# Modulation weights with 256 columns of all four chunks in a piece, and layer 1's second and third group at the end of layer 0's experts

## The chip, the cores and the metric

The kernel runs on one core of a Trainium2 chip. Its engines are TensorE (PE in the profile; PEld is its weight load), VectorE (DVE), ScalarE (ACT), GpSimd (POOL) and SyncE (SP), which here issues nearly all DMAs. The metric is device time in microseconds (us). Before the change it is 2171.39 us, the median of three runs (2170.97 to 2172.95).

## The reference

Two layers of a transformer-like block work on 256 latent tokens and 256 context tokens of 1024 channels. Only the latents come out, so layer 1 computes queries for them alone. Everything is float32.

```python
for l in range(2):
    sh1, sc1, g1, sh2, sc2, g2 = split(silu(c) @ w_mod[l] + b_mod[l], 6)      # w_mod[l]: [1024, 6144]
    csh1, ..., cg2             = split(silu(c_ctx) @ w_mod[l] + b_mod[l], 6)  # the same weights, the context's vector
    h = layer_norm0(x) * (1 + sc1) + sh1                     # context tokens with csc1, csh1
    z = h @ w_in[l] + b_in[l]                                # columns for three mixers and their gates
    y = (sum over attention, GLA, neighbourhood of sigmoid(gate) * (branch @ w_br)) @ w_out[l]
    x = layer_norm(alpha * x + g1 * y)
    h2 = layer_norm0(x) * (1 + sc2) + sh2
    x = layer_norm(alpha * x + g2 * moe(h2))                 # 32 experts, two of them for each token
```

The change concerns the first two lines: a product of two vectors (c and c_ctx) with 25 MB of weights a layer, whose six results of 1024 columns scale, shift and gate the tokens. sh1 and sc1 are needed at the start of a layer, the others from its out_norm on.

## The kernel before

Tokens lie on the partitions in tiles of 128: four tiles in layer 0, two query tiles in layer 1. A layer runs through norm_T (normalisation, transposition, modulation), two GLA pairs (each for two heads of the gated linear attention), attention, neighbourhood attention, merges, out_norm, routing, the experts, a loop for tokens beyond the experts' slots, and final_norm.

**Modulation.** `modulation(l, groups)` makes 2048 of a layer's 6144 columns, called a group: four chunks of 512 columns. Group 0 holds shift and scale of the first norm, groups 1 and 2 the rest. The two vectors stand in `sT` as the 32-column stationary operand (30 columns are zero), and chunk j's result goes to rows 32 j to 32 j + 31 of one PSUM bank `mod`, that is to one of four column quarters of TensorE. The weights come in pieces of [128, 1024], 512 KB each, 16 for a group (eight steps over the 1024 rows, two halves). A piece holds 512 columns of two chunks, so each step's first piece serves quarters 0 and 1, the second 2 and 3. In the trace a float32 product is two instructions. Then VectorE adds the bias (`mg`, line 500), TensorE transposes `mg` (`modT`, line 503), VectorE takes columns from it (`mU`, line 517), and `mg` of groups 1 and 2 is stored to device memory as `md` (line 520), from which rows are read later (line 529). Called with the tag "tmod", the same tiles have the names `tmod` and `tmodT`.

**Where the groups stand.** Layer 0: group 0 at the start, groups 1 and 2 with the first and the second GLA pair. Layer 1: group 0 at the end of layer 0's out_norm, group 1 behind layer 1's norm_T, group 2 with its second GLA pair. In a GLA pair the scores G are made in six steps, between which VectorE works (`Sd`, line 732); other TensorE work fills the gaps.

**The end of layer 0.** Each expert has six tiles of 1 MB of weights; they come through six "ew" buffers and two "ewb" buffers. The last experts' second products Y (line 1414) and the combines `cb` (lines 1428 and 1429) are followed by sums on VectorE and GpSimd (lines 1431 and 1432, tile `ct` from two buffers). Then `overflow` reads a count and runs a loop over as many blocks (line 1545); with the inputs here it runs no block. All engines meet at the loop's head. Behind it come final_norm (lines 1589 to 1600), with its loads `lgb`, and layer 1.

**What sets the order.** Each engine runs its instructions in a fixed order, and so does SyncE with its DMAs. The order is made when the program is built, by a scheduler that follows the order of the source and may move work forward where its own estimate finds a gap. Nothing is moved across the loop's head. A tile from a pool waits until the instructions that use the buffer's former tile are done.

Of the kernel before, what the change touches and what calls it, by code (L numbers as in the profile page):

```python
# [21 lines left out]
NL = 2  # L22
# [5 lines left out]
# columns of w_in  # L28
A_Q, A_K, B_Q, B_K, B_V, B_R, B_A, C_Q, C_K, C_V, GATE = 0, 512, 768, 1024, 1280, 1792, 2304, 2336, 2848, 3360, 3872

# the order in which the mixers' weights stream in, one [128, 1024] piece each
# [27 lines left out]
# columns of the per-partition biases  # L59
# [9 lines left out]
# sections of the constants  # L69
# [9 lines left out]
# ranks of the experts of layer 0, by load but for experts 0 and 1, whose weights come in early:  # L79
# with 128 slots, with 64, the others with 32; the order of their halves of 128 slots  # L80
# [29 lines left out]
def groups(l):  # L110
    """The experts (in layer 0 by rank of their load) that share 256 slots, in two halves of one, two or four experts"""
# [10 lines left out]
def _constants():  # L122
# [5 lines left out]
    i = np.arange(128)  # L128
# [14 lines left out]
    # slots of the experts by rank  # L143
# [15 lines left out]
    # pairs of tokens of a block of 64 whose highest different bit is the level's  # L159
# [5 lines left out]
def _layout(inp):  # L165
    """The arrays of setup_inputs() as the program reads them."""
# [6 lines left out]
    # w_mod: [layer, group of four 512-column chunks, k tile, half of the group][partition][2 chunks x 512]  # L173
    wm = g["w_mod"].reshape(NL, 8, 128, 3, 2, 1024)
    o["wmod"] = np.ascontiguousarray(wm.transpose(0, 3, 1, 4, 2, 5))
# [8 lines left out]
    # branches in the order in which they are merged: gla, attention, neighbourhood  # L184
# [42 lines left out]
    # the relative bias of every (query, key), outside of the window a constant; context keys have none  # L227
# [12 lines left out]
    # experts: [layer, expert][partition][six pieces of 2048]  # L240
# [9 lines left out]
class _Prog:  # L250
# [3 lines left out]
    # ---- tiles  # L254
# [14 lines left out]
    def rsqrt(self, v, w, tmp=None):  # L269
        """v ** -0.5 by Newton's method"""  # L270
# [18 lines left out]
    def split(self, src, hi, lo, eng=None):  # L289
        """hi + lo = src, exactly, each with 12 significant bits"""  # L290
        self.nc.scalar.copy(hi, src)  # L291
        (eng or self.nc.vector).tensor_tensor(lo, src, hi.bitcast(F32), op=ALU.subtract)  # L292

    def stats(self, x):
        """mean and 1 / sqrt(var + eps) of x [128, 1024]"""
# [9 lines left out]
    def norm0(self, x, xh, total=None):  # L305
        """xh = layer_norm0(x), both [128, 1024]; with the sums of x, ScalarE makes those of its squares"""
# [15 lines left out]
    def stats_all(self, xs, apart=False):  # L322
        """stats of tiles together: columns of means, of 1 / sqrt(var + eps), and of the opposites of their products"""
# [25 lines left out]
    def norm_quick(self, x, out, g, b):  # L349
        """out = layer_norm0(x) * g + b, on VectorE alone, and the sums of its rows; x is overwritten"""  # L350
# [7 lines left out]
    def norm(self, x, out, g, b, last=None):  # L358
        """layer_norm0(x) * g + b, in two steps"""
# [4 lines left out]
    # ---- streams of weights  # L364
    def raw(self, l):
        """A place for weights as they come in; the first ones of layer 1 can't wait for the tokens that use the others"""
# [17 lines left out]
    def projT(self, l, n, ntok):  # L384
        """[128 columns of w_in, tokens] = w^T h^T"""
# [7 lines left out]
    def projM(self, l, names, kper, width, tiles, sub=None):  # L393
        """[tokens, columns of w_in] for the token tiles, one bank each"""
# [17 lines left out]
    # ---- constants  # L412
# [42 lines left out]
    def open(self, name, side, tags):  # L455
        """A pool that shares its place with the one that follows it on the same side"""
# [6 lines left out]
    @contextmanager  # L463
    def later(self, n=400):
        """What is traced here gives way to the next n instructions"""
        self.tc.cur_priority += n
        yield
        self.tc.cur_priority -= n

    # ---- modulation  # L470
    def modulation(self, l, groups, tag="raw", tag2="b2", ps="mod"):
        """[128, 512] of group g: row 32 j + s holds 512-column chunk 4 g + j for the latents (s = 0) and the context (s = 1)"""
# [11 lines left out]
        for g in groups:  # L484
            p = self.ps(ps)
            for k in range(8):
                if tag == "ew":
                    raw = self.t([128, 2, 1024], tag, name="wmod")
                    raws = [raw[:, h] for h in range(2)]
# [1221 lines left out]
```

## Time and profile before

| | before |
|---|---|
| time, median of 3 runs | 2171.39 us |
| profiled execution, span | 2169.8 us |
| TensorE busy | 1989.3 us (92%) |
| VectorE / ScalarE / GpSimd busy | 968.1 / 561.9 / 272.2 us |
| modulation products `mod` / `tmod`, busy | 75.0 / 20.0 us |
| modulation pieces loaded | 96 of 512 KB |

For the profiled execution the span is the only time of its own; what the runs time beyond it is the difference to their median, 1.6 us. Shares of busy time are means over stages with different limits, so a change in one stage is read from that stage's rows.

### The profile page before, as it was taken

Reading aid. Unit: us, or ns where it says so; the run is one execution under the profiler, and the core shown is the slowest. Engines: PE = TensorE matmul, PEld = TensorE weight load, DVE = VectorE, ACT = ScalarE, POOL = GpSimd, SP = SyncE. Lnnn points to the kernel's source line nnn. Section 1 sums busy time; section 2 is a strip of 40 time slices with the busy share of each in tenths; the row PEclk is TensorE's granted clock in tenths of the full one; section 3 lists DMA queues with packets and bytes.
Section 4 is the critical chain, followed back from the end, with each engine's and each line's share of the span. In section 5 each row is a group of like instructions: output and inputs, shape, how many; then the busy total and the mean of one; then the engine's idle time right before and its main releaser. Section 6 shows DMA issues by size and latency. Waiting matters only on the chain. (4 is left out here: it accounts for less than half of the span.)

```text
span 2169.8 us, 28061 instructions
## 1 busy us (share of the span) xinstructions
PE 1989.3 (92%) x10749; PEld 1179.2 (54%) x10749; DVE 968.1 (45%) x2236; ACT 561.9 (26%) x992; POOL 272.2 (13%) x260
## 2 busy tenths in 40 slices
PE   5999999999998898989899598999996999999995
PEld 2676766777885353445253165786795433333321
DVE  4676765564388131222022765766648222221213
ACT  3443334343333000000000254444543111010000
POOL 1322100011110010111011222100020000000000
PEclk9999999999999999999999798999997999999998
DMA  7436212223328899999998723632466999999995
GB/s 289 164 121 218 78 59 69 93 83 96 126 79 334 367 420 421 371 385 421 419 369 370 270 85 112 197 118 74 139 207 250 387 421 423 421 423 422 421 422 222
DMA packets 113987, 562.41 MB, mean 259 GB/s; under 512 B 13302, under 2 KB 14838, under 8 KB 72120
## 3 DMA queue, kind: packets, MB, share of 16 engines
q1 hardware_dynamic: 113272, 558.85, 66.9%
q8 instruction: 87, 1.43, 0.3%
q10 hardware_dynamic: 576, 1.70, 0.2%
q14 instruction: 52, 0.43, 0.1%
HBM read 557.36 MB, written 3.15 MB: 258 GB/s over the span
## 5 line engine op out<-in xcount | busy, mean ns | idle before, releaser
L1506 PE MATMUL h<-ew,XT 128*64 128x512 f32 (+2 forms) x2048 | 478.3, 611 | 40.0 <-DMA ew<-in_ew_dram 39.8
L1506 PEld LDWEIGHTS h<-ew,XT 128*64 128x64 f32 (+2 forms) x2048 | 146.6, 135 | 326.3 <-issue 248.8
L1414 PE MATMUL Y<-ew,aT 128*64 128x512 f32 (+2 forms) x1024 | 252.4, 598 | 10.1 <-DMA ew<-in_ew_dram 7.9
L292 DVE TENSOR_TENSOR wlo<-raw,whi 128x1024 fp32r<-128x1024 f32 (+1 forms) x140 | 178.9, 1278 | 139.6 <-ACT whi L291 138.4
L1432 POOL TENSOR_TENSOR x<-x,ct 128x512 f32<-128x512 f32 x82 | 105.0, 1307 | 1003.5 <-DVE ct L1431 879.8
L380 PE MATMUL pT<-hThi,whi 128*128 128x512 f32 (+1 forms) x576 | 202.9, 352 | 1.5 <-ACT whi L291 0.8
L291 ACT CAST whi<-raw 128x1024 fp32r<-128x1024 f32 (+1 forms) x140 | 145.4, 1039 | 226.5 <-PE pT L381 116.2
L382 PE MATMUL pT<-hThi,wlo 128*128 128x512 f32 (+1 forms) x576 | 202.3, 351 | 0.2 <-DVE wlo L292 0.2
L381 PE MATMUL pT<-hTlo,whi 128*128 128x512 f32 (+1 forms) x576 | 202.1, 351 | 0.0
L1403 DVE SCALAR_TENSOR_TENSOR act<-h,s,sl 128x512 f32<-128x512 f32 x30 | 22.5, 751 | 325.4 <-PE h L1506 270.5
L1414 PEld LDWEIGHTS Y<-ew,aT 128*64 128x64 f32 (+2 forms) x1024 | 76.0, 133 | 151.0 <-issue 125.7
L807 DVE TENSOR_TENSOR Yl<-Y,Yh 128x512 fp32r<-128x512 f32 x60 | 41.4, 690 | 257.2 <-ACT Yh L806 254.1
L806 ACT CAST Yh<-Y 128x512 fp32r<-128x512 f32 x60 | 35.2, 587 | 462.5 <-PE Y L1414 462.5
L380 PEld LDWEIGHTS pT<-hThi,whi 128*128 128x128 f32 x576 | 109.5, 190 | 22.4 <-issue 4.1
L382 PEld LDWEIGHTS pT<-hThi,wlo 128*128 128x128 f32 x576 | 109.5, 190 | 16.2 <-issue 2.9
L381 PEld LDWEIGHTS pT<-hTlo,whi 128*128 128x128 f32 x576 | 109.6, 190 | 15.2 <-issue 3.0
L380 PE MATMUL pM<-whi,hThi 128*128 128x512 f32 (+1 forms) x304 | 110.7, 370 | 3.6 <-ACT qTkT L645 1.9
L381 PE MATMUL pM<-wlo,hThi 128*128 128x512 f32 (+1 forms) x304 | 111.8, 369 | 0.0
L382 PE MATMUL pM<-whi,hTlo 128*128 128x512 f32 (+1 forms) x304 | 111.7, 368 | 0.0
L495 PE MATMUL mod<-wmod,sT 128*32 128x512 f32 x320 | 75.0, 624 | 23.4 <-DVE s L343 14.8
L1407 ACT COPY aT<-aT 128x512 f32<-128x512 f32 x30 | 17.6, 586 | 292.7 <-PE aT L1406 292.7
L1383 PE MATMUL XT<-OH,h2hi 128*128 128x256 f32 x352 | 89.1, 290 | 0.0
(363 smaller groups left out, 3093.4 us busy)
## 6 DMA issues: line engine op xcount, KB each, us to landing
ew<-in_ew_dram SPq DMA_DIRECT2D x326, 1024.0 KB, 13.8
raw<-in_w_dram SPq DMA_DIRECT2D x145, 512.0 KB, 3.7
ew<-in_ew_dram SPq DMA_DIRECT2D x116, 512.0 KB, 13.5
wmod<-in_wmod_dram SPq DMA_DIRECT2D x96, 512.0 KB, 6.1
nb<-in_nb_dram SPq DMA_DIRECT2D x32, 256.0 KB, 3.8
g<-md SPq DMA_DIRECT2D x12, 256.0 KB, 7.6
row<-in_ln_dram SPq DMA_DIRECT2D x4, 512.0 KB, 4.9
lgb<-in_ln_dram SPq DMA_DIRECT2D x4, 512.0 KB, 12.0
```

The source lines that it names most:

```text
L291: self.nc.scalar.copy(hi, src)
L292: (eng or self.nc.vector).tensor_tensor(lo, src, hi.bitcast(F32), op=ALU.subtract)
L380: mm(out, lh, rh, start=start, stop=False)
L381: mm(out, lh, rl, start=False, stop=False)
L382: mm(out, ll, rh, start=False, stop=stop)
L495: nc.tensor.matmul(p[32 * j:32 * j + 32, :], self.sT[:, k, :], raws[j // 2][:, 512 * (j % 2):512 * (j % 2) + 512], start=k == 0, stop=k == 7)
L806: self.nc.scalar.copy(hi, src)
L807: self.nc.vector.tensor_tensor(lo, src, hi.bitcast(F32), op=ALU.subtract)
L1383: mm(p[:, w * j:w * j + w], self.h2s[t][part][:, 128 * k:128 * k + 128], OH[:, t], start=t == 0 and part == 0, stop=t == T - 1 and part == 1)
L1414: mm(y[m * i:m * i + m, :], aT[:, 128 * f + m * i:128 * f + m * i + m], w2(f, n, i), start=f == 0, stop=f == 3)
L1432: (nc.vector if last and n else nc.gpsimd).tensor_tensor(self.x1[t][:, ns], self.x1[t][:, ns], tmp, op=ALU.add)
L1506: mm(h[m * i:m * i + m, :], XTs[dp][:, k, 128 * pr + m * i:128 * pr + m * i + m], w[i, 2 * q + k // 4][k % 4], start=k == 0, stop=k == 7)
```

## The change

Three things change, and line numbers from 487 on grow by two or three. The layout of `wmod` in device memory: a piece now has 256 columns of each of the four chunks. `modulation` runs over 16 such pieces, first the eight with the left halves of the chunks, then those with the right halves, with four products of 256 columns each. And layer 1's groups 1 and 2 leave their places and are made together behind layer 0's experts, in front of the overflow loop, with their weights in "ew" buffers (two pieces to a buffer) and bias and sum in "ct" buffers.

```diff
-    wm = g["w_mod"].reshape(NL, 8, 128, 3, 2, 1024)
-    o["wmod"] = np.ascontiguousarray(wm.transpose(0, 3, 1, 4, 2, 5))
+    wm = g["w_mod"].reshape(NL, 8, 128, 3, 4, 2, 256)
+    o["wmod"] = np.ascontiguousarray(wm.transpose(0, 3, 5, 1, 2, 4, 6)).reshape(NL, 3, 2, 8, 128, 1024)
...
         for g in groups:
             p = self.ps(ps)
-            for k in range(8):
+            for i in range(16):
+                h, k = i // 8, i % 8
                 if tag == "ew":
-                    raw = self.t([128, 2, 1024], tag, name="wmod")
-                    raws = [raw[:, h] for h in range(2)]
+                    if k % 2 == 0:
+                        both = self.t([128, 2, 1024], tag, name="wmod")
+                    raw = both[:, k % 2]
                 else:
-                    raws = [self.t([128, 1024], tag if isinstance(tag, str) else tag[2 * k + h], name="wmod") for h in range(2)]
-                for h in range(2):
-                    nc.sync.dma_start(raws[h], self.a["wmod"][l, g, k, h])
+                    raw = self.t([128, 1024], tag if isinstance(tag, str) else tag[i], name="wmod")
+                nc.sync.dma_start(raw, self.a["wmod"][l, g, h, k])
                 for j in range(4):
-                    nc.tensor.matmul(p[32 * j:32 * j + 32, :], self.sT[:, k, :], raws[j // 2][:, 512 * (j % 2):512 * (j % 2) + 512],
+                    nc.tensor.matmul(p[32 * j:32 * j + 32, 256 * h:256 * h + 256], self.sT[:, k, :], raw[:, 256 * j:256 * j + 256],
                                      start=k == 0, stop=k == 7)
...
             self.norm_T(l, xs)
             if l:
-                self.modulation(1, [1], "o4", "b2", "tmod")
-            if l:
                 self.vectors(l)
...
             for p in range(2):
                 self.gla_pair(l, p, T)
-                if l == 0 or p == 1:
+                if l == 0:
                     self.modulation(l, [1 + p])
...
             self.experts(l, T)
             if l:
                 lgb = self.final_loads(l)
+            else:
+                self.modulation(1, [1, 2], "ew", "ct", "tmod")
             self.overflow(l, T)
```

SyncE at the end of layer 0's experts, before: the last tiles of the experts' weights (`ew`), the loop's branch, then the loads of final_norm (`lgb`) and the first pieces of layer 1's group 1 (`wmod`).

```order
L1463 DMA ew_8666<-in_ew_dram 128x1024
L1463 ISA
L1463 DMA ew_8669<-in_ew_dram 128x1024
L1463 ISA
L1463 DMA ew_8669<-in_ew_dram 128x1024
L1545 COMPARE_AND_BRANCH
...
L1611 DMA lgb_9051<-in_ln_dram 128x1024
L1611 DMA lgb_9052<-in_ln_dram 128x1024
L493 DMA wmod_9238<-in_wmod_dram 128x1024
```

The same place on SyncE now; `bm` is a group's bias, `md` its store.

```order
L1465 DMA ew_8797<-in_ew_dram 128x1024
L495 DMA wmod_8904<-in_wmod_dram 128x1024 x2
L495 DMA wmod_8915<-in_wmod_dram 128x1024 x2
...
L500 DMA bm_8992<-in_bmod_dram 128x512
L495 DMA wmod_9007<-in_wmod_dram 128x1024 x2
...
L522 DMA md_9004<-mg_8994 128x512
L500 DMA bm_9095<-in_bmod_dram 128x512
L495 DMA wmod_9073<-in_wmod_dram 128x1024 x2
L495 DMA wmod_9084<-in_wmod_dram 128x1024 x2
L522 DMA md_9106<-mg_9097 128x512
L1547 COMPARE_AND_BRANCH
```

All 32 pieces (16 rows of two), both biases and both stores now stand in front of the loop's branch; `lgb` comes behind it, with no `wmod` after it.

TensorE at the same place, before: the last combine and the loop's head.

```order
L1428 MATMUL cb_8767<-Yh_8683,C_8708 128x512
L1429 MATMUL cb_8767<-Yl_8684,C_8708 128x512
L1544 TENSOR_LOAD r_5_5991
L1545 COMPARE_AND_BRANCH
```

TensorE there now.

```order
L1430 MATMUL cb_8895<-Yh_8811,C_8836 128x512
L1431 MATMUL cb_8895<-Yl_8812,C_8836 128x512
L497 MATMUL tmod_8903<-wmod_8904,sT 32x256 x8
...
L497 MATMUL tmod_8903<-wmod_8981,sT 32x256 x8
L505 MATMUL tmodT_8996<-cst,mg_8994 128x128 x4
L497 MATMUL tmod_9006<-wmod_9007,sT 32x256 x8
...
L497 MATMUL tmod_9006<-wmod_9084,sT 32x256 x8
L505 MATMUL tmodT_9099<-cst,mg_9097 128x128 x4
L1546 TENSOR_LOAD r_5_6119
L1547 COMPARE_AND_BRANCH
```

None of the modulation's products stands in front of a combine, and both groups with their transposes stand in front of the loop.

TensorE in layer 1's second GLA pair, before, from its start: the pieces of group 2 (`mod`) among the states' products (`kET`, `dS`) and the scores (`G`).

```order
L495 MATMUL mod_10383<-wmod_10393,sT 32x512 x2
L682 MATMUL kET_10128<-cst,EK_10115 128x128 x4
L495 MATMUL mod_10383<-wmod_10400,sT 32x512 x2
L690 MATMUL dS_10135<-V_9972,kE_10133 64x128 x8
L682 MATMUL kET_10145<-cst,EK_10115 128x128 x4
L495 MATMUL mod_10383<-wmod_10401,sT 32x512 x2
L495 MATMUL mod_10383<-wmod_10408,sT 32x512 x2
L690 MATMUL dS_10152<-V_9972,kE_10150 64x128 x8
...
L703 MATMUL G_10193<-YX_10195 64x64 x4
L495 MATMUL mod_10383<-wmod_10409,sT 32x512 x2
L703 MATMUL G_10194<-YX_10195 64x64 x4
```

There now; `pM` with 256 columns are attention projections.

```order
L381 MATMUL pM_10646<-wlo_10707,hThi_9493 128x256
L684 MATMUL kET_10382<-cst,EK_10369 128x128 x4
L382 MATMUL pM_10646<-whi_10706,hTlo_9497 128x256
...
L380 MATMUL pM_10649<-whi_10706,hThi_9492 128x256
L692 MATMUL dS_10389<-V_10226,kE_10387 64x128 x8
L684 MATMUL kET_10399<-cst,EK_10369 128x128 x4
...
L692 MATMUL dS_10406<-V_10226,kE_10404 64x128 x8
L705 MATMUL G_10418<-qTkT_10190 64x64
...
L705 MATMUL G_10447<-YX_10449 64x64 x4
L705 MATMUL G_10448<-YX_10449 64x64 x4
L705 MATMUL G_10418<-YX_10430 64x64 x4
```

The 96 projections that followed the pair now stand around its states' products, and nothing stands between the steps of G.

## Rows read from the trace of the kernel before

**Rows 1.** The page: busy time of each engine, share of the span, instructions.
```profile
PE 1989.3 (92%) x10749; PEld 1179.2 (54%) x10749; DVE 968.1 (45%) x2236; ACT 561.9 (26%) x992; POOL 272.2 (13%) x260
```

**Rows 2.** Timeline of SyncE from 1165: start, duration, engine, line, operation, count.
```profile
1168.11 8.47 SPq L1463 DMA_DIRECT2D ew<-in_ew_dram  x7
1207.38 0.82 SPq L1611 DMA_DIRECT2D lgb<-in_ln_dram  x2
```

**Rows 3.** Waits of SyncE, 1150 to 1260: line, releaser, total us, times, longest.
```profile
SPq L1545 <- remote: 26.6, 1, 26.6
```

**Rows 4.** Windows: length, busy PE, PEld, DVE, ACT, POOL, clock, DMA share, GB/s.
```profile
1164.00:1166.00 2.00, 2.00 (x9) 1.01 (x10) 0.79 (x2) 0.00 (x0) 1.99 (x2) 1.00 1.01 422
...
1186.00:1188.00 2.00, 2.00 (x10) 0.76 (x9) 1.35 (x2) 0.59 (x1) 0.00 (x0) 1.00 0.56 211
...
1206.00:1208.00 2.00, 0.00 (x0) 0.00 (x0) 0.90 (x2) 0.00 (x0) 0.00 (x0) 0.50 0.02 4
```

**Rows 5.** Timelines of TensorE and VectorE around the loop's head; in brackets idle before.
```profile
1194.46 3.65 PE L1414 MATMUL Y<-ew,aT 128*64 128x512 f32 x8
...
1201.83 0.39 PE L1429 MATMUL cb<-Yl,C 128*128 128x512 f32 x1
...
1206.24 0.69 DVE L1432 TENSOR_TENSOR x<-x,ct 128x512 f32<-128x512 f32 x1
1208.65 4.84 DVE L336 BATCH_NORM_STATS2 s<-x 128x6 f32<-128x512 f32 x8 [1.71 <-issue]
```

**Rows 6.** Timelines behind the loop (ScalarE, VectorE, TensorE); landing of the md stores.
```profile
1237.65 4.63 ACT L539 ACTIVATE xh<-x,s 128x1024 f32<-128x1024 f32 x4 [16.13 <-DVE s L346]
...
1252.32 0.68 DVE L500 TENSOR_TENSOR mg<-tmod,bm 128x512 f32<-128x512 f32 x1
...
1253.06 0.66 PE L503 MATMUL tmodT<-cst,mg 128*128 128x128 f32 x4 [1.48 <-DVE mg L500]
...
DMA to landing us min/median/max: 2.0/6.3/14.2
```

**Rows 7.** Windows in layer 1's first norm, columns as in rows 4.
```profile
1235.00:1240.00 5.00, 1.06 (x4) 0.72 (x4) 2.84 (x29) 2.35 (x3) 0.00 (x0) 0.50 1.02 407
...
1245.00:1250.00 5.00, 5.00 (x29) 1.98 (x28) 3.81 (x6) 5.00 (x10) 2.40 (x2) 1.00 0.49 189
```

**Rows 8.** TensorE in layer 1's second pair; window of line 495: length, PE, PEld, clock, DMA.
```profile
1339.63 1.92 PE L495 MATMUL mod<-wmod,sT 128*32 128x512 f32 x16
...
1345.36 1.09 PE L690 MATMUL dS<-V,kE 128*64 128x128 f32 x16
...
1382.37 0.28 PE L382 MATMUL pM<-whi,hTlo 128*128 128x256 f32 x1
1382.49 0.40 PE L380 MATMUL pM<-whi,hThi 128*128 128x512 f32 x1
...
1290.00:1370.00 80.00, 14.63 (x64) 2.06 (x64) 0.89 0.41 135
```

**Rows 9.** TensorE in layer 1's first pair: G from its start, then projections.
```profile
1301.91 0.46 PE L703 MATMUL G<-qTkT 64*64 64x64 f32 x16
...
1311.31 0.79 PE L380 MATMUL pM<-whi,hThi 128*128 128x512 f32 x1
...
1312.33 0.63 PE L382 MATMUL pM<-whi,hTlo 128*128 128x512 f32 x1
```

**Rows 10.** TensorE in layer 0: G and a lone piece in the first pair, experts' products.
```profile
96.71 0.69 PE L703 MATMUL G<-qTkT 64*64 64x64 f32 x32
...
105.64 1.05 PE L495 MATMUL mod<-wmod,sT 128*32 128x512 f32 x4 [0.71 <-DMA wmod<-in_wmod_dram]
...
726.90 7.91 PE L1506 MATMUL h<-ew,XT 128*32 128x512 f32 x66
```

**Rows 11.** Windows in layer 0's first GLA pair, columns as in rows 4.
```profile
92.00:96.00 4.00, 3.33 (x35) 1.87 (x36) 2.48 (x2) 1.75 (x3) 3.48 (x3) 1.00 0.97 368
...
100.00:104.00 4.00, 3.81 (x44) 1.26 (x44) 3.57 (x9) 2.08 (x2) 1.12 (x2) 1.00 0.86 284
```

## The prediction

> **What bounds the kernel now.** I read the head of the page first: TensorE is busy for 92% of the span, so time is lost or won mainly where TensorE waits or does work that another engine could not overlap [rows 1]. Its sum says nothing of where, so I went to the two stretches that the change touches and to the stretch that it moves work into.
>
> The end of layer 0's experts. SyncE's timeline shows the last expert weights issued at 1168.1 us, then nothing until 1207.4 [rows 2]. Its waits put 26.6 us of this on line 1545, the head of the overflow loop, with "remote" as the releaser: it stands at the loop's barrier until the other engines arrive [rows 3]. DMA by windows moves 422 GB/s while the weights come, half of that in the window from 1186 to 1188, and 4 GB/s still in the one from 1206 to 1208 [rows 4]. That is a hole of some 20 us, from about 1187. Meanwhile TensorE finishes second products to 1198.1 and combines to 1202.2, VectorE adds the last result until 1206.93, and ScalarE, SyncE and VectorE all start again between 1207.4 and 1208.7 [rows 5]. So the barrier opens about 0.45 us after the last engine's last work, and nothing passes it.
>
> Behind the barrier come final_norm and layer 1's first norm: VectorE and ScalarE work, with layer 1's group 1 on TensorE beside them as its weights land [rows 6]. From 1245 to 1250 ScalarE is busy 5.00 of 5 us, so this stretch is its and VectorE's [rows 7].
>
> Layer 1's second GLA pair. Here TensorE starts group 2 at 1339.6, mixes its pieces with the scores G, and is through the attention projections of 256 columns that follow at 1382.5 [rows 8]. Layer 0's two pairs mix groups 1 and 2 with their G in the same way [rows 10].
>
> **The hole does not hold what is put into it.** A group is 16 pieces of 0.524 MB, 8.39 MB; two are 16.78 MB. At the expert weights' 422 GB/s [rows 4] a piece takes 1.24 us, a 1 MB tile 2.49, two groups 39.8 us. Without a gap from 1187 on, they would end at 1226.8, 19 us after the barrier opens now. And there is a gap. The tiles come from the six "ew" buffers, which the last experts' products still read: the last of them comes free with the last second product at 1198.1 [rows 5]. So tiles 1 to 6 land by about 1202.8. The seventh needs a tile that the modulation itself has used, and its matmuls stand behind all combines, so the first is used up at about 1203.3; issue and landing cost some 2 us (the md write's fastest landing is 2.0 us [rows 6]), so DMA is idle for about 2.5 us. Ten tiles (25 us), two biases and the two md stores (0.26 MB each, 0.6 us) end at about 1232. After that the last piece's products (0.6), the sum mg (0.68 [rows 6]), the md store (at least 2.0 to land, and SyncE's branch stands behind it) and 0.45 for the barrier: about 1236 instead of 1207.4, **+28.5 us**. The bounds: +24 (no gap: 1226.8 + 1.3 + 2.0 + 0.45 is 1230.6, and 0.8 for the biases), and +33 (ten tiles in 30 us instead of 25, at 350 GB/s, near the better of the GLA stretches' rates [rows 11]). Only the first 20 us of this had been DMA idle; nothing hides the rest, because VectorE, ScalarE and GpSimd have no other work in front of the barrier and final_norm sits behind it.
>
> **What the two old places give back.** After the barrier, group 1 no longer stands among layer 1's first transposes. Gone are TensorE's wait for mg of 1.48 us and mg's 0.68 on VectorE, which also makes the norm's low parts [rows 6]: about 2 us. On the other side TensorE loses the products that occupied it as the weights came. Its granted clock was 0.50 from 1235 to 1240 even with them and 1.00 from 1245 [rows 7]; if it comes back later, the norm's transposes and the gate projections run up to twice as long for some us. I take 0, bounds -3 and +3. The first four layer-1 weights come by ScalarE's queue and have less beside them, which no one waits for.
>
> In the second GLA pair the group's products take 14.63 us, and the pair runs 42.9 us from 1339.63 to 1382.49. Without them, the order puts 96 attention projections of 256 columns among the states' products in front of G (0.12 us from one start to the next, 11.5 us; today they stand behind G). The states' products, two dS of 1.09 us [rows 8] and what is between them, take 3.4. G alone takes 9.4 us in layer 1's first pair, 1301.9 to 1311.3 [rows 9]. The output products and their waits I estimate at 6 us. Sum 30.3, plus a loss of clock: behind the same G without filler the first pair's projections of 512 columns take 0.63 us [rows 9] where one takes 0.40 otherwise [rows 8]; eight of these are 1.8 us. So 32 against 42.9: **-10.5 us**, rounded. Bounds: -14.6, all of the group's product time, and -6, if what G waits for (VectorE's Sd) is uncovered fully twice.
>
> **The new form of a piece.** Now a piece holds two chunks, so its four instructions (two per chunk in the trace) use two of the four column quarters. Alone, such a piece takes 1.05 us [rows 10], while four pieces back to back take 1.92, 0.12 us an instruction [rows 8]. The experts' products, four quarters side by side, also step by 0.12 (66 in 7.91 us) [rows 10]. With 256 columns of all four chunks, a lone piece is eight instructions of half the length. If they run four abreast it is 8 x 0.055, about 0.45, plus 0.15 to drain: 0.6. That short ones can follow each other so fast is shown by dS, 16 in 1.09 us [rows 8]. The upper bound is 0.12 an instruction: 0.96 alone, and 3.8 for four back to back where 1.92 stands. In layer 0's two GLA pairs some 10 pieces a group run alone or in twos. 0.45 each would be 4.5 us, but weights are nearly late as it is: DMA is busy 0.86 to 0.97 there [rows 11] and TensorE waits for a piece, once 0.71 us [rows 10]. I take 3 us a pair (0 to 5). The group at the start is paced by DMA (0.4), layer 1's group 0 lies among the router's logits at the end of out_norm, where its last pieces precede the routing: 1.6 (0 to 3). Together **-8 us** in layer 0 (-13 to 0; +4 if the instructions do not overlap).
>
> The Trainium skill, "TensorEngine Tiling (Array Packing)", Instruction Overhead, gives each matmul about 60 cycles on trn2, and warns against taking the tiling from a dimension that is already small. By it 64 more instructions a group at 2.4 GHz would cost an estimated 1.6 us, some 6 us in the four groups that stay. The G rows with 64 columns, 0.015 us apart [rows 10], speak against such a cost side by side, and the sum above goes without it.
>
> **Sum.** +28.5 - 10.5 - 8 + 0 = +10 us on the profiled execution's span of 2169.8, that is 2179.8. The median of the runs is 2171.39, 1.6 above that span, so I forecast **2181.4 us**.
>
> **Rivals.**
> 1. *The barrier does not hold final_norm.* If only SyncE and TensorE waited for the modulation, its weights would run beside final_norm and the norm (30 us until xh at 1237.7 [rows 6]), and only the gains stay: 2171.4 - 18.5 = 2153. For it: the modulation's results are needed only from out_norm on. Against it: all engines restart within 1.3 us of one another, SyncE after 26.6 us of waiting [rows 2, 3, 5]. This decides if VectorE leaves the loop's head while SyncE is still issuing. 5%.
> 2. *Break-even.* The gains reach their upper bounds (-14.6 in the pair, -11 in layer 0) and DMA runs without a gap (+25): 2171. For it: the last buffer of the experts is free at 1198.1, 5 us before the sixth tile would have landed. Against: each gain is at its bound at once. 20%, a third of it below the old time.
> 3. *The modulation's weights come slower than the experts'.* In the GLA pairs the same pieces came at 284 to 368 GB/s [rows 11]: 33 instead of 28.5, and a cold TensorE behind the barrier +3: 2189. Against: after the barrier they came at 407 [rows 7]. 15%.
> The Trainium skill, "DMA: Bandwidth & Descriptors", Specifications, has a limit of about 358 GB/s of HBM for a core; by it 16.8 MB would take an estimated 46.9 us, and this rival would be the forecast. The 422 GB/s of the expert weights [rows 4] exceed it, so here the rows decide.
> 4. *The new form does nothing*, a piece of eight costs 0.96 us: the instructions have a price of their own, whatever their length. Layer 0 then gives 0 and the result is 2189, 2193 where back-to-back pieces get slower; at the end of the experts DMA's pace hides it. For it: 0.12 us an instruction in two kinds of products [rows 8, 10]. Against: dS and G. 12%.
>
> **Numbers.** The forecast has 48%, and its own range is 2175 to 2188. About what a measurement of this kernel can tell from no change is 0.2%, 4.3 us: faster means below 2167.1, slower above 2175.7. Faster: rival 1 and a third of rival 2, 0.11. Same: half of rival 2 and the forecast's lower edge, 0.14. Slower: 0.75. The range reaches from 2169, in the middle of rival 2, to 2193, 4 us beyond rivals 3 and 4.
>
> **What would show it.** DMA at about 420 GB/s from 1187 to 1232 with one gap near 1203; SyncE's wait at the loop nearly gone, that of VectorE and ScalarE for it new, 28 us long; final_norm's first statistics near 1237 instead of 1208.7 and xh the same 29 us behind it; from the start of layer 1's second pair to the attention projections' end about 32 us instead of 42.9; a lone piece at 0.6 us in layer 0 and modT 3 us earlier in each pair. If final_norm starts before the last tmod product, the forecast falls; if lone pieces still take 1 us, the layer 0 term does.

## The result, and the profile after

The changed kernel takes 2195.36 us (median of four runs, 2192.6 to 2197.53) against 2171.18 before; the ratio is 1.0107, with a 95% interval of 1.0088 to 1.0126. It is some 24 us slower, where 10 were forecast, and 2 us beyond the range. The profiled execution has a span of 2193.3 us, 23.5 more than before.

The page: TensorE does less work in more time.

```profile
PE 1985.0 (91%) x11133; PEld 1197.4 (55%) x11133; DVE 967.7 (44%) x2236; ACT 560.6 (26%) x992; POOL 271.5 (12%) x260
```

The place that [rows 2] showed, SyncE after the last expert weights (start, duration, instruction, count; in two pieces of the timeline).

```profile
1174.08 28.36 SPq L495 DMA_DIRECT2D wmod<-in_wmod_dram  x16
...
1233.62 0.33 SPq L522 DMA_DIRECT2D md<-mg  x1
1236.23 0.97 SPq L1613 DMA_DIRECT2D lgb<-in_ln_dram  x2
```

It now issues weights where it stood waiting, and the loop's head is passed at 1236.2 instead of 1207.4. Its wait at the loop, 26.6 us in [rows 3], is 1.0 us for the md store. ScalarE waits instead: the waits from 1150 to 1270 have 52.9 us for it, in front of its first work in final_norm.

```profile
ACT x L1598 <- DVE s L346: 52.9, 1, 52.9
...
SPq L1547 <- DMA md<-mg: 1.0, 1, 1.0
```

In the kernel before it waited 18.1 us in the same place (waits from 1150 to 1260).

```profile
ACT x L1596 <- DMA raw<-in_w_dram: 18.1, 1, 18.1
```

The windows of the same stretch, to compare with [rows 4] (length, busy PE, PEld, DVE, ACT, POOL, clock, DMA share, GB/s).

```profile
1184.00:1188.00 4.00, 4.00 (x19) 1.60 (x18) 1.10 (x2) 0.33 (x1) 0.00 (x0) 1.00 1.01 404
...
1200.00:1204.00 4.00, 4.00 (x80) 2.44 (x76) 3.96 (x7) 0.00 (x0) 0.01 (x1) 1.00 0.63 200
...
1220.00:1224.00 4.00, 3.36 (x28) 0.59 (x24) 0.00 (x0) 0.00 (x0) 0.00 (x0) 0.50 1.02 405
1224.00:1228.00 4.00, 2.18 (x19) 0.42 (x19) 0.00 (x0) 0.00 (x0) 0.00 (x0) 0.50 1.05 415
1228.00:1232.00 4.00, 3.48 (x28) 0.79 (x32) 0.00 (x0) 0.00 (x0) 0.00 (x0) 0.50 0.51 203
```

DMA runs at 399 to 415 GB/s through the former hole and 23 us beyond it, with one gap around 1200 to 1204, where the next tiles wait for TensorE to use up the first. From 1208 to the barrier ScalarE and GpSimd do nothing, and VectorE only the sums `mg` and the short copies `mU`. TensorE's timeline there, and behind it VectorE's in front of the barrier, answer to [rows 5].

```profile
1199.20 0.39 PE L1431 MATMUL cb<-Yl,C 128*128 128x512 f32 x1
1199.56 5.82 PE L497 MATMUL tmod<-wmod,sT 128*32 128x256 f32 x104
...
1224.15 1.08 PE L497 MATMUL tmod<-wmod,sT 128*32 128x256 f32 x8 [0.19 <-DMA wmod<-in_wmod_dram]
...
1227.98 1.08 PE L497 MATMUL tmod<-wmod,sT 128*32 128x256 f32 x8 [1.48 <-DMA wmod<-in_wmod_dram]
...
1230.53 2.31 PE L497 MATMUL tmod<-wmod,sT 128*32 128x256 f32 x16 [0.19 <-DMA wmod<-in_wmod_dram]
```

```profile
1232.90 0.69 DVE L502 TENSOR_TENSOR mg<-tmod,bm 128x512 f32<-128x512 f32 x1 [20.60 <-PE tmod L497]
...
1237.21 4.85 DVE L336 BATCH_NORM_STATS2 s<-x 128x6 f32<-128x512 f32 x8 [2.17 <-issue]
```

Thirteen pieces follow at once on the last combine (104 instructions in 5.82 us, 0.06 each, as dS in [rows 8] suggested). Then a piece comes every 1.28 us, and TensorE at half clock takes 1.08 for it. final_norm starts at 1237.21, where 1208.65 stood.

A program's executions differ by several microseconds in some stages and by nothing in others, so the account is made by stages and over several profiles. Each was cut at starts or ends in the timelines: layer 0 to the transposition of layer 1's group 0 (A), to the end of layer 0's last combine (B), to the first statistics of final_norm (C), to the gate products of layer 1's second pair (D), to the first transposes of attention's keys (`kTs`; E), to VectorE's last instruction, some 3 us before the span's end (F). Layer 1's gate products of the second pair run in front of the first pair's G, so E holds both pairs. Two profiles each of before and after, one of each experiment (the rows' names are those of the sections below):

| us | A | B | C | D | E | F |
|---|---|---|---|---|---|---|
| before | 683.3, 682.6 | 519.0, 519.1 | 6.4, 6.4 | 78.9, 80.4 | 103.1, 99.5 | 775.7, 776.1 |
| after | 680.6, 675.6 | 519.0, 519.4 | 37.6, 38.3 | 80.7, 83.6 | 94.1, 93.5 | 778.2, 778.3 |
| form alone | 676.6 | 519.1 | 6.4 | 80.3 | 97.8 | 779.9 |
| move alone | 685.3 | 520.5 | 38.2 | 83.5 | 91.0 | 778.8 |
| one group moved | 678.8 | 518.4 | 15.6 | 82.5 | 97.0 | 781.0 |
| behind, old form | 686.8 | 520.8 | 6.4 | 99.7 | 92.6 | 777.6 |
| behind, new form | 677.5 | 519.6 | 6.4 | 89.1 | 94.0 | 778.3 |
| behind, old form, no weights | 687.3 | 520.2 | 6.4 | 89.3 | 91.1 | 780.2 |
| mixed form | 673.8 | 516.2 | 5.9 | 79.4 | 94.5 | 779.9 |
| mixed form, warm products | 675.6 | 517.4 | 5.9 | 84.1 | 97.4 | 777.9 |
| after, warm products | 672.9 | 520.9 | 37.9 | 83.3 | 91.0 | 778.7 |
| after, filler in the pair | 680.3 | 518.8 | 37.7 | 81.0 | 96.8 | 777.9 |

### The profile page after: what moved, and what is told of

Read it like the earlier page. It is cut to its first block, busy times and chain, and to the rows that moved or that the text cites. A ratio compares the mean times of both kernels' runs of the same rounds, so it can differ in the third digit from the quotient of the medians.

```text
span 2193.3 us, 28832 instructions
## 1 busy us (share of the span) xinstructions
PE 1985.0 (91%) x11133; PEld 1197.4 (55%) x11133; DVE 967.7 (44%) x2236; ACT 560.6 (26%) x992; POOL 271.5 (12%) x260
## 5 line engine op out<-in xcount | busy, mean ns | idle before, releaser
L1416 PE MATMUL Y<-ew,aT 128*64 128x512 f32 (+2 forms) x1024 | 251.9, 598 | 10.8 <-DMA ew<-in_ew_dram 8.6
L1385 PE MATMUL XT<-OH,h2hi 128*128 128x256 f32 x352 | 89.3, 290 | 0.2 <-DVE OH L1363 0.2
L1385 PE MATMUL XT<-OH,h2lo 128*128 128x256 f32 x352 | 87.1, 284 | 0.0
## 6 DMA issues: line engine op xcount, KB each, us to landing
ew<-in_ew_dram SPq DMA_DIRECT2D x116, 512.0 KB, 13.5
```

The costliest lines, as they stand in the source:

```text
L1385: mm(p[:, w * j:w * j + w], self.h2s[t][part][:, 128 * k:128 * k + 128], OH[:, t], start=t == 0 and part == 0, stop=t == T - 1 and part == 1)
L1416: mm(y[m * i:m * i + m, :], aT[:, 128 * f + m * i:128 * f + m * i + m], w2(f, n, i), start=f == 0, stop=f == 3)
```

## The experiments

All are made from the kernel before; "form" is the new layout with 256-column products, as in the diff of the change.

**The form alone**, all groups at their old places.

```diff
...
-                    nc.sync.dma_start(raws[h], self.a["wmod"][l, g, k, h])
...
+                nc.sync.dma_start(raw, self.a["wmod"][l, g, h, k])
...
```

> The new form of the pieces alone; all six groups stay where they stood before. Theory 'form cools': the changed kernel's trace has layer 0's last combine only 2.65 us earlier than before, although every lone piece is 0.4 us shorter, because TensorE's granted clock falls to 0.56 behind the first group (1.00 before). The same has to show here: norm_T of layer 0 again some 3.7 us late, the last combine 2 to 3.5 us early, group 2 of layer 1 shorter by up to 3 us; about 2167 in all (-3 to -6). Rival 'reordered': the loss at the start comes from what the scheduler did elsewhere because of the moved groups; then the clock stays at 1.00 at the start and the form gives the 8 us of the prediction and some 3 in layer 1: 2160.

Measured: 2163.73 us, ratio 0.9956 (0.9941 to 0.997): 9.5 us faster, more than the first theory's -3 to -6, about the rival's 10. Each theory was half right. The clock did fall at the start: 0.85 from 36 to 54 us, and the gate products started at 53.3 instead of 51.7. But layer 0 gained 6.7 us by the end of stage A. Lone pieces in its GLA pairs take 0.64 us, as in this row of the changed kernel, where [rows 10] has 1.05:

```profile
97.93 0.64 PE L497 MATMUL mod<-wmod,sT 128*32 128x256 f32 x8 [1.11 <-DMA wmod<-in_wmod_dram]
```

**The move alone**, pieces in the old form.

```diff
-                self.modulation(1, [1], "o4", "b2", "tmod")
...
-                if l == 0 or p == 1:
+                if l == 0:
...
+            else:
+                self.modulation(1, [1, 2], "ew", "ct", "tmod")
             self.overflow(l, T)
```

> The move alone; pieces in the old form (512 columns of two chunks). Theory 'the barrier holds it': layer 0 as before up to the last combine, then from there to the first statistics of final_norm some 34 to 37 us instead of 6.4 (changed kernel: 37.6), since DMA sets the pace whatever the form is; TensorE stays warm on the longer products, so up to 1.5 us less at the end; layer 1's second pair gives back 5 to 7: 2171 + 30 - 6 = 2195. Rival 'the new form makes the end slow' (its products run at half clock there): with old products the end costs the 28.5 of the prediction or less, and the pair gives the 10.5: 2189.

Measured: 2196.74 us, ratio 1.0106 (1.009 to 1.0123). Stage C is 38.2 us with the old products as with the new ones, 1 us above the expected range, so the form is not what makes the end slow, and that rival falls. With the longer products TensorE's clock stays at 1.00 there, where it was 0.50 in the changed kernel; a piece takes 1.05 us instead of 1.08, and the stage is no shorter.

```profile
1228.00:1232.00 4.00, 3.33 (x14) 0.43 (x12) 0.00 (x0) 0.00 (x0) 0.00 (x0) 1.00 1.03 409
```

Against the form alone, the changed kernel shows what the move costs under the new form: 1.0107 / 0.9956, or 33 us; here, under the old form, 23.

**One group moved**: new form, group 1 at the experts' end, group 2 left in the second pair.

```diff
-                self.modulation(1, [1], "o4", "b2", "tmod")
...
+            else:
+                self.modulation(1, [1], "ew", "ct", "tmod")
             self.overflow(l, T)
```

> New form; only group 1 goes to the end of the experts, group 2 stays in layer 1's second pair. Theory 'DMA's pace behind the hole': 8 of the 16 tiles; six land before the combines end, two come after the gap, so the barrier opens about 7 us later than without (from the last combine 12 to 13 us instead of 5.2), against 31.5 for two groups; layer 0 gives -2.65, the shorter group 2 up to -3: 2171 to 2175. Rival 'each group costs the same': half of 31.5, so 2171 + 15.7 - 5 = 2182.

Measured: 2176.72 us, ratio 1.002 (1.0009 to 1.0031). Its last pieces on TensorE, the start of final_norm on VectorE, and the first load behind the loop on SyncE:

```profile
1204.64 0.64 PE L496 MATMUL tmod<-wmod,sT 128*32 128x256 f32 x8 [0.69 <-DMA wmod<-in_wmod_dram]
1207.34 1.08 PE L496 MATMUL tmod<-wmod,sT 128*32 128x256 f32 x8 [2.06 <-DMA wmod<-in_wmod_dram]
```

```profile
1212.80 1.29 DVE L336 BATCH_NORM_STATS2 s<-x 128x6 f32<-128x512 f32 x2 [2.18 <-issue]
```

```profile
1211.93 1.20 SPq L1612 DMA_DIRECT2D lgb<-in_ln_dram  x2
```

Stage C is 15.6 us, 9.1 over before, against 31.2 and 31.9 for two groups. The second group's 8.39 MB thus cost 22.1 to 22.8 us there; at 405 GB/s they take 20.7. The first one costs 9.1 although the hole is as long as its transfer, for the gap and the chain behind the last landing. The theory of DMA's pace holds, though it had put 12 to 13 us from the last combine to the barrier's opening, where 14.7 stand (`lgb`), and that of equal costs falls; the time is 2 us above the range.

**Both groups behind the barrier**, old form: group 2 follows group 1 behind layer 1's norm_T.

```diff
-                self.modulation(1, [1], "o4", "b2", "tmod")
+                self.modulation(1, [1, 2], "o4", "b2", "tmod")
...
-                if l == 0 or p == 1:
+                if l == 0:
```

> Old form; groups 1 and 2 of layer 1 both stand behind layer 1's norm_T, that is behind the loop's barrier and beside final_norm, where group 1 stood. Theory 'it is the barrier, not the bytes': the barrier opens as before (5.2 us after the last combine); the weights come in the 30 us of VectorE and ScalarE work behind it; layer 1's second pair gives back 5 to 7 us, and up to 4 are lost because the second group's products are among the first projections: 2165 to 2171. Rival 'the bytes': the 8.4 MB delay whatever they are put in front of, so the weights of the first projections come 20 us later and the time is 2180 or more.

Measured: 2183.48 us, ratio 1.0049 (1.0031 to 1.0067). The barrier opens as before (C is 6.4), but D grows by about 20 us. TensorE's timeline and the window of the products' line from the first to the second gate products (length, PE, PEld, clock, DMA share, GB/s):

```profile
1275.12 1.05 PE L495 MATMUL tmod<-wmod,sT 128*32 128x512 f32 x4
...
1303.64 1.05 PE L495 MATMUL tmod<-wmod,sT 128*32 128x512 f32 x4
```

```profile
1269.12:1313.68 44.56, 13.68 (x52) 1.88 (x52) 0.96 0.42 129
```

Thirteen lone pieces stand among projections that keep TensorE busy without a break, and take 13.7 us of it, while DMA is at 129 GB/s. So the time is 12 us above the theory's range and in that of its rival, but not for the rival's cause: the place behind the barrier is not free either, and what it costs in this stretch is TensorE's time, not an arrival.

**The same without group 2's weights**: its products all read group 1's last two pieces.

```diff
...
-                for h in range(2):
+                for h in range(2) if (l, g) != (1, 2) else ():
                     nc.sync.dma_start(raws[h], self.a["wmod"][l, g, k, h])
...
```

> Old form, groups 1 and 2 of layer 1 both behind layer 1's norm_T, as in the experiment before, but group 2's weights are left out: its 64 products all read the last two pieces of group 1. Theory 'the bytes': from layer 1's first gate products to the second pair's gate products it took 44.6 us there against 27.1 before; without the 8.4 MB it falls to 27 to 35 (the products alone are 16 pieces of 0.48 us), and the time from 2183 to 2165 to 2172. Rival 'the products and their order': these stand in front of the projections as before, so it stays at 40 or more, 2178 or more.

Measured: 2175.32 us, ratio 1.0022 (1.0011 to 1.0034). Between the two sets of gate products it takes 29.2 us, as the bytes' theory had it, but the first gate products come 4.9 us later than with the loads: the products have only moved in front of them. Over both, 10.4 of the 20 us are gone. With nothing to wait for, the 16 pieces run back to back, at 0.44 us each instead of 1.05, which is most of it:

```profile
1259.97 7.07 PE L496 MATMUL tmod<-wmod,sT 128*32 128x512 f32 x64
```

So neither theory as written was right, and the time is above the first one's range.

**The same place in the new form**, with all weights: the two diffs of places and form together, in short

```diff
-                for j in range(4):
-                    nc.tensor.matmul(p[32 * j:32 * j + 32, :], self.sT[:, k, :], raws[j // 2][:, 512 * (j % 2):512 * (j % 2) + 512],
+                for j in range(4):
+                    nc.tensor.matmul(p[32 * j:32 * j + 32, 256 * h:256 * h + 256], self.sT[:, k, :], raw[:, 256 * j:256 * j + 256],
...
-                self.modulation(1, [1], "o4", "b2", "tmod")
+                self.modulation(1, [1, 2], "o4", "b2", "tmod")
```

> New form, groups 1 and 2 of layer 1 both behind layer 1's norm_T. In the old form this cost 11 us: from layer 1's first gate products to the second pair's gate products 44.6 us instead of 27.1, TensorE busy all the time, with 13 lone pieces of group 2 at 1.05 us among the projections. Theory 'lone pieces where TensorE is full': the same pieces now take 0.64 us, so this stretch is 36 to 40 us, layer 0 gives its 7 us as in the other kernels with the new form, and the time is 2183.5 - 7 - 5 to 7, 2169 to 2172: no better than the new form with the groups at their old places (2163.7). Rival 'the bytes': the weights' arrival sets that stretch, it stays at 43 or more, 2176.

Measured: 2170.00 us, ratio 0.9996 (0.9985 to 1.0007). The stretch is 37.7 us and its lone pieces take 0.64:

```profile
1270.88 0.64 PE L496 MATMUL tmod<-wmod,sT 128*32 128x256 f32 x8
```

Both numbers are where the theory of lone pieces put them; the bytes' rival (43 or more) falls.

**Before and after again**, unchanged.

> The kernel before, unchanged, profiled a second time, to see how far stages of one program differ between executions. Theory 'layer 0 gains from the form, and single profiles scatter': three profiles with the new form end layer 0's routing (first modT behind out_norm) at 676.6 to 680.6 us, two with the old form at 685.3 and 686.8, the first one of before at 683.3; this one should lie between 682 and 688, and its stretch from layer 1's first attention transposes to its first logits nearer to the 274 to 275 of all other runs than to the 271.7 of the first profile. Rival 'the changed kernel's layer 0 gains only 2.7 us': this one is at 683 or below, with 271.7 again.

> The changed kernel, unchanged, profiled a second time. Theory 'scatter': layer 0's routing ends anywhere between 676 and 681 us, and the stretch from the last combine to final_norm's first statistics is again 37.6 us within 0.7, because DMA's rate sets it. Rival 'that stretch scatters as much': it is off by 3 us or more.

Measured: 2169.31 and 2193.42 us, each once; the spans are 2167.5 and 2191.6, 24.1 apart, as the medians are. Stage C is fixed within 0.7 us, as expected; stages A, D and E scatter by up to 5 (A of after ends 0.4 us below its expected range). The last stretch of layer 0's routing in the two runs of after, and in the first one of before:

```profile
680.58 0.66 PE L505 MATMUL modT<-cst,mg 128*128 128x128 f32 x4 [0.83 <-DVE mg L502]
```

```profile
675.58 0.66 PE L505 MATMUL modT<-cst,mg 128*128 128x128 f32 x4 [0.83 <-DVE mg L502]
```

```profile
683.27 0.66 PE L503 MATMUL modT<-cst,mg 128*128 128x128 f32 x4 [0.79 <-DVE mg L500]
```

Over all profiles made here the old form ends stage A at 682.6 to 687.3 us (five, mean 685.1), the new form throughout at 672.9 to 680.6 (seven, mean 677.5): 7.6 us. The second profile of before alone decides nothing: its 682.6 us fit the theory (682 to 688) and the rival (683 or below) alike, and its attention, 272.9 us from the first transposes to the first logits, lies between the 271.7 of the first profile and the 274 that was expected. What speaks for the theory is the two sets of profiles.

**Layer 0's first group in the old form**, all else as in the form alone.

```diff
+                two = l == 0 and g == 0
+                h, k = (i % 2, i // 2) if two else (i // 8, i % 8)
...
```

> The new form with all groups at their old places, but layer 0's first group, at the start of the program, in the old form (512 columns of two chunks). Theory 'form cools': there the weights' arrival sets the pace, so shorter pieces gain nothing and only leave TensorE idle; with the old form the granted clock behind it is 1.00 instead of 0.6 and layer 0's gate products start at 51 to 52.5 us instead of the 53.3 and 55.4 of the two profiles with all groups in the new form: 1 to 3 us less than the form alone, 2161 to 2163. Rival 'the clock there is chance': no difference from the form alone, 2163.7 within 1, and the gate products at 53 or later.

Measured: 2161.05 us, ratio 0.9957 (0.9943 to 0.9971). The gate products start at 51.8 us and the clock from 36 to 52 is 0.89, as before, so in that place the long products keep TensorE's clock. Stage A ends at 673.8 us here and at 675.6 in the other profile of this form (below), where the new form throughout has a mean of 677.5. In the time the two forms can't be told apart (0.9956 and 0.9957).

**Warm products in front of layer 1's transposes**, in the changed kernel.

```diff
+            if l:
+                self.warm(14, xs[3][:, :128])
             self.norm_T(l, xs)
```

> The changed kernel with 14 more products of 256 columns (28 instructions) in front of layer 1's transposes, made from final_norm's last tile, which nothing reads. They stand where group 1 stood, without its weights. Theory 'the clock behind the barrier': in the last 21 us before layer 1's gate products the granted clock was 0.76 and 0.80 in the changed kernel (0.92 before), and from there to the second pair's gate products it took 28.6 and 30.2 us (27.1 and 28.6 before). With the warm products the clock is 0.9 or more and the stretch from final_norm's first statistics to the second pair's gate products falls by 2 to 5 us from 80.7 and 83.6: 2190 to 2193. Rival 'the order of VectorE and ScalarE': the clock follows, the stretch stays within 1 us, no change.

Measured: 2192.67 us, ratio 1.0106 (1.0089 to 1.0122). The stretch is 83.3 us, within the 80.7 to 83.6 of the changed kernel.

```profile
1256.85 8.99 PE L1169 MATMUL warm<-cst,x 128*128 128x256 f32 x28 [27.57 <-DVE x L1599]
1265.67 1.04 PE L551 MATMUL hT<-cst,xh 128*128 128x128 f32 x8
```

The products ended where the transposes begin, the clock of the last 21 us before the gate products rose only to 0.84, and nothing was gained: the theory of the cold clock behind the barrier is not borne out. Since the clock did not reach the 0.9 that the theory asked for, it is not ruled out either, and what makes D some 2.5 us longer stays open.

**The same in the kernel with the mixed form.**

```diff
+                two = l == 0 and g == 0
...
+                self.warm(14, xs[3][:, :128])
```

> All groups at their old places in the new form but layer 0's first one in the old form (2161.05 before, ratio 0.9957), with the 14 warm products in front of layer 1's transposes. Theory 'the clock behind the barrier': there the clock before the gate products was 0.85 and the next stretch 29.3 us; with them 1 to 3 us less, 2158 to 2160. Rival: within 1 us of 2161, or later because the warm products stand in front of group 1's.

Measured: 2164.14 us, ratio 0.9973 (0.9961 to 0.9985). Nothing gained here either; the first gate products come 4.8 us later after the barrier than without.

**Filler in the second pair** of the changed kernel: group 2's products without its weights.

```diff
+                elif p == 1:
+                    q = self.ps("mod")
+                    for i in range(16):
+                        for j in range(4):
+                            nc.tensor.matmul(q[32 * j:32 * j + 32, :256], self.sT[:, i % 8, :], self.c["iota"], start=True, stop=True)
```

> The changed kernel with 64 more products (128 instructions of 256 columns) in layer 1's second GLA pair, from a constant, which nothing reads: group 2's products without its weights. Theory 'cooling took the gain': from the end of the first pair to the first attention scores the changed kernel takes 44.1 and 45.0 us at a clock of 0.81 and 0.77 (51.5 and 50.9 at 0.97 and 1.00 before; 47.0 at 1.00 with the new form and group 2 in place). With the filler the clock is 0.95 or more, and the filler's own time is paid back: 42 to 46 us, no worse than without. Rival 'the products' time counts': the stretch grows by half of their 7.7 us or more, to 48 us and above, 2199.

Measured: 2195.52 us, ratio 1.0113 (1.0098 to 1.0128). From the first pair's end to attention's first transposes (the expectation calls them scores), by windows, in before, after, this one, the mixed form with group 2 in place, and the form alone (columns as above):

```profile
1339.23:1390.68 51.45, 47.18 (x400) 31.22 (x400) 30.73 (x100) 18.71 (x42) 11.68 (x18) 0.97 0.69 230
```

```profile
1367.98:1412.08 44.10, 39.20 (x332) 33.40 (x332) 26.71 (x93) 17.60 (x42) 11.50 (x18) 0.81 0.16 55
```

```profile
1367.72:1414.48 46.76, 44.48 (x461) 35.41 (x460) 26.31 (x95) 17.59 (x42) 11.99 (x18) 0.89 0.16 51
```

```profile
1322.72:1369.71 46.99, 40.92 (x466) 30.91 (x465) 29.62 (x101) 18.85 (x43) 9.91 (x18) 1.00 0.73 250
```

```profile
1329.85:1380.22 50.37, 44.71 (x465) 33.05 (x464) 30.13 (x101) 18.28 (x42) 10.78 (x18) 0.90 0.68 233
```

128 more instructions cost 1.8 to 2.7 us, not their 7.7, and the clock is 0.89 instead of 0.77 to 0.81. That lies between the two expectations (0.95 and no cost; 48 us): part of the products' time is paid back. They also ran in TensorE's idle time, which fell from 4.9 to 2.3 us, and the run doesn't part that from the quicker clock. A group 2 with its weights costs this stretch 2 to 3 us in the profile of the mixed form, at a clock of 1.00. In the form alone, the one group moved and the mixed form with warm products the stretch has 50.0 to 50.5 us at 0.90, so there it costs 5 to 6. The clock goes with the length; that it alone decides is not shown.

## Why the prediction was wrong

Its direction and its mechanism were right: two groups don't fit into the hole, the barrier holds final_norm, and the end of the experts costs more than the two old places and the form give back. Rival 1 is ruled out by stage C, rival 2 by the gains, which stayed well below their bounds, rival 4 by the 0.64 us of a lone piece, rival 3's slow weights by 399 to 415 GB/s. Rival 3's other half, 3 us for a cold TensorE behind the barrier, is near what stage D shows, but its cause was not confirmed.

Wrong is the size, +24 for +10. The step that failed is the sizing of the sum's terms: four came out 2.5 to 3 us worse than put, a fifth stage was not in the sum, and all missed in the same direction. By stage, forecast and measured, the latter as the difference of the means over two profiles each:

| us | A | B | C | D | E | F | sum |
|---|---|---|---|---|---|---|---|
| forecast | -8 | 0 | +28.5 | 0 | -10.5 | none | +10 |
| measured | -4.9 | +0.2 | +31.5 | +2.5 | -7.5 | +2.3 | +24.1 |

The end of the experts, put at +28.5 us, measured +31.2 and +31.9 (C). Of the 3 us, 1 to 2 are weights: TensorE waits for a piece until 1230.53 and then runs the last two without another wait, so the last one landed 31 to 32 us after the last combine, and the forecast's 1232 is 30 behind it. A piece came every 1.28 us, not 1.24, which makes 0.8 over the 20 pieces behind the gap. The store and the bias between the last tiles, for which TensorE waits 1.48 us at 1227.98 while DMA keeps its 415 GB/s, had been counted. The rest is mainly TensorE at half clock, which took 2.31 us over the last two pieces, where 0.6 for one was reckoned. The gap near 1203 and the chain of mg, store and barrier came about as worked out.

The second pair, put at -10.5 (its own sum, 32.1 against 42.9, makes -10.8), measured -5.9 to -7.4 by the windows from the first pair's end (51.45 and 50.90 us before, 44.10 and 44.97 after); stage E, with the first pair in it, has -5.4 to -9.6. The projections moved forward and G without filler came as the order had it; the clock was under-priced. In the 44 us it was 0.77 and 0.81, and the output products `o` and projections behind G ran at half clock (0.63 us a projection, as [rows 9] had shown for the first pair):

```profile
1382.95 0.46 PE L705 MATMUL G<-qTkT 64*64 64x64 f32 x16
...
1392.14 1.23 PE L705 MATMUL G<-YX 64*64 64x64 f32 x16 [0.54 <-DVE Sd L734]
1393.65 0.79 PE L758 MATMUL o<-V,S 128*128 128x128 f32 x2 [0.28 <-POOL S L742]
...
1401.14 0.79 PE L380 MATMUL pM<-whi,hThi 128*128 128x512 f32 x1
...
1402.16 0.63 PE L382 MATMUL pM<-whi,hTlo 128*128 128x512 f32 x1
```

The output products in the kernel before:

```profile
1365.85 0.49 PE L756 MATMUL o<-V,S 128*128 128x128 f32 x2
...
1370.18 0.71 PE L758 MATMUL o<-st,EQ 64*128 64x128 f32 x4
```

From G's start to the outputs it took 10.7 us, where 9.4 were reckoned, and the outputs took 7.5, where 6 were reckoned and 5.0 stood before. The clock's price had been put on the eight projections alone.

The norm behind the barrier and the first projections, put at 0 within 3, took 80.7 and 83.6 us instead of 78.9 and 80.4 (D), about +2.5, near the upper bound; the cause stays open.

The form in layer 0, put at -8, is -7.6 over all profiles, so this term held within the scatter; between the profiles of the two kernels themselves it is -2.0 to -7.7, and between the two first ones only -2.7, because the one of after was late and the one of before early. Stage F, not spoken of, is 2 us longer. It is so in every edited kernel, with whatever edit (777.6 to 781.0), so it does not hang on the move; its cause was not found.

The range failed with the sum. Nearly every term lies inside its own bounds, but the range let only one thing go wrong at a time: the unfavourable bounds together (+33, +3, -6 and 0) make +30, some 2201 us, and it ended at 2193.

No gain was counted twice: the form's -8 was for layer 0 alone, and the pair's -10.5 was taken against the pair in the old form. But the parts of the change don't add up. The form alone gains 9.5 us and the move alone costs 23, together 13.5, and both in one cost 23. Part of this is stage E: with group 2 in place it is 94.5 to 97.8 us in the new form (four profiles) and 103.1 and 99.5 in the old, and without group 2 it is 94.1 and 93.5 in the changed kernel, so under the new form there is less to give back. Against the form alone the move costs 33 us. A version that beats both kernels is the form with all groups where they stood: 2163.73 us, 0.4% below the kernel before.

## What to carry to other kernels

Before work is put into a transfer's idle time in front of a barrier, count its bytes against the hole and add the chain behind the last landing: what exceeds the hole is paid in full, since nothing behind the barrier can cover it (here about 22 us for a second group whose transfer takes 20.7). An edit with two parts is priced one after the other: what the first makes cheap, the second can't save again. A range has to allow several terms to miss the same way at once. And one profile per kernel does not settle a term of a few microseconds; a second profile of the unchanged kernel showed which stages scatter.

## What the runs showed that was not expected

Shorter products can cost time in a stretch where the weights set the pace. At the start of the program, with pieces arriving every 1.25 us, two-chunk pieces kept TensorE at a clock of 1.00 up to 36 us; in the new form it was 0.56 from 32 to 36 in the changed kernel (0.50 to 0.88 in the other profiles), and the gate products came up to 3.7 us later than in the first profile of before. Over all profiles they start at 51.9 to 55.4 us with that group in the new form and at 50.6 to 52.5 with it in the old one.

The windows of before and after:

```profile
32.00:36.00 4.00, 2.78 (x16) 0.94 (x15) 1.02 (x2) 0.41 (x1) 0.00 (x0) 1.00 0.99 335
```

```profile
32.00:36.00 4.00, 2.17 (x16) 0.40 (x16) 0.21 (x1) 0.40 (x1) 0.00 (x0) 0.56 0.92 330
```

A piece of eight short instructions takes 0.64 us at full clock and 1.08 at half, where the long form took 1.05 at full clock: most of the form's gain is lost while the clock is down. In the kernel's time this is not clear of noise: the mixed form gained no more than the form alone.
